# A hybrid SSD / RWKV-7 encoder layer on one core: the state space norm's weight factors folded into the output weight's rows, its token factors multiplied in on GpSimd, four empty turns behind the first load, and the group norm's second product tied behind the chain's

## The chip, the cores and the metric

The kernel runs on one core of a Trainium2 chip. That core has a matrix engine (TensorE, PE in the profile), a vector engine (VectorE, DVE), a scalar engine (ScalarE, ACT), a general engine (GpSimd, POOL), a queue engine that issues nearly all transfers here (SyncE, SP; its instruction stream is "SPq" in the trace) and 16 DMA engines. Each engine executes its own instructions strictly in the order in which they were written into its stream; an instruction that waits holds up everything behind it. The metric is the device time of one execution in microseconds (us); the median of three runs counts.

## What is computed

One layer over 2,048 tokens of width 1,024. One projection feeds two groups of heads: a bidirectional Mamba-2 state space model (SSD, 512 channels) and a bidirectional RWKV-7 recurrence (512 channels). Their outputs side by side go through one 1024x1024 output projection, and an MLP follows. The parts that matter here:

```python
# end of ssd_bidir: RMS norm over each half (256 channels), times a weight per channel
y = (y * silu(z)).reshape(b, T, G, SSD_WIDTH // G)
y = y * rsqrt(mean(y * y, -1, keepdims=True) + RMS_EPS)
y_ssd = y.reshape(b, T, SSD_WIDTH) * norm_g
# end of rwkv7_bidir: group norm over each head of 64 channels
mu_y = mean(y, -1, keepdims=True);  var_y = mean(square(y - mu_y), -1, keepdims=True)
y = ((y - mu_y) * rsqrt(var_y + GN_EPS)).reshape(b, T, W) * lnx_g + lnx_b
y_rwkv = (y + bonus) * g
# hybrid_mixer
mix = concatenate([y_ssd, y_rwkv], -1) @ w_out
h = layer_norm(ALPHA * h + mix, ln1_g, ln1_b)
h = layer_norm(ALPHA * h + square(relu(h @ w_fc)) @ w_proj, ln2_g, ln2_b)
```

Products are made in fp32 precision from halves: an operand x is split into xh (rounded by ScalarE) and xl = x - xh, and three products (xh·wh, xh·wl, xl·wh) are summed in PSUM.

## The kernel before

Three stretches follow one another: projections and state space scan (to about 1,050 us), the RWKV stretch (about 1,060 to 1,970 us), and the MLP (to the end). The change touches the second alone.

The RWKV stretch runs through 32 *units* u (16 chunk pairs for two groups of heads). `weave(chain(u), jobs)` writes the instructions: after each step of `chain(u)`, the serial recurrence, it draws steps from the jobs beside it: `finish(u - 1)` (group norm of finished chunks), `merge(u + 1)`, `inverse(u + 2)` (a triangular inverse, row by row, all on GpSimd: lines 1059 to 1066) and `prep(u + 3)`. Such a job is an entry with a number of steps to be drawn per unit (12 for `finish`).

The chain of one unit makes, twice (c = 0, 1), three small products on PE (all on line 1150, told apart by their operands): `ch<-zv,kr`, then `ch<-rs,nm` (rs is ScalarE's negated copy, line 1166), then `ch<-zv,bkt`; the last one's result is added on VectorE to the state: `zt` (line 1189) at c = 1. The next unit of the same group starts from zv, made from zt.

Between those products, `dense(ins, n)` fills PE with large ones: it adds n to a credit and, while the credit is 1 or more, draws a *piece* of three 128x512 matmuls from `out_pieces`, and ties it behind the given instruction with `tc.issue_after`. A piece generator that yields `HELD` ends that turn and caps the credit at 1. `out_pieces` makes, in this order: gates for blocks 1 and 2; `weights(0)`, which loads the first 512 rows of w_out and splits them (woh, wol; lines 807 and 808); the state space norm's token factors (rt, written to DRAM as rsD, line 891); then the *first pass* of the output projection over 16 token tiles, 8 pieces each, in `products` (line 838); then `weights(4)`, gates for blocks 0 and 3, and the *second pass* for the RWKV half.

`load(t, k.yS, True)` fetches a token tile of the unnormed state space output for the first pass (yr from yS, line 818), fetches the factors of its 128 tokens broadcast over partitions (rsb from rsD, line 821), and scales yr by the weight's factor per channel and the token's factor with four VectorE instructions (line 823). ScalarE then rounds it to yh (line 825) and GpSimd makes yl (line 827). The load for tile j+1 is written when tile j's products begin. In `weights`, ppc(k, "ng", i // 2) would be the column of `norm_g` that belongs to the row block i // 2: partitions there are channels, as they are in yr.

In `finish`, each of two chunks per unit takes a centring product (line 1223), a copy ye (1224) and a square sq on ScalarE (1226), a second product over sq for the variance (line 1230, vp), and then sd (1233), reciprocal and the rest.

What order these streams end up in is decided by a scheduler that goes by an estimated timeline and takes every instruction as soon as its inputs and the ties allow; a small edit can so move rows of all engines.

Of the kernel before, what the change touches and what calls it, by code (L numbers as in the profile page):

```python
# [11 lines left out]
AF = mybir.ActivationFunctionType  # L12
ALU = mybir.AluOpType
# [3 lines left out]
P = 128  # L17
# [23 lines left out]
C_ID, C_MU, C_ML, C_MLX, C_ONE, C_BLK, C_HSEL, C_N = 0, 128, 256, 384, 512, 640, 768, 770  # L41
# [75 lines left out]
FL = 0.4  # L117
FH = 1.0
# [84 lines left out]
def ppc(k, name, j):  # L203
    c = _PP[name] + j
    return k.pp[:, c:c + 1]
# [576 lines left out]
DENSE, HELD, LAST, END = "dense", "held", "last", object()  # L782


def out_pieces(k):


    nc, tc, I = k.nc, k.tc, k.I
    with ExitStack() as ctx:
# [3 lines left out]
        def weights(c0):  # L793
            wh, wl = [cp.tile([P, 4, D], F32R, name=n) for n in ("woh", "wol")]

            def raw(i):
                w = wk.tile([P, 4, P], F32, name="yr").rearrange("p a t -> p (a t)")
                r = (c0 + i // 2) * P
                nc.sync.dma_start(w, I["w_out"][r:r + P, 512 * (i % 2):512 * (i % 2) + 512])
                return w  # L800

            w = raw(0)
            yield
            for i in range(8):
                nxt = raw(i + 1) if i < 7 else None
                cs = wh[:, i // 2, 512 * (i % 2):512 * (i % 2) + 512], wl[:, i // 2, 512 * (i % 2):512 * (i % 2) + 512]
                nc.scalar.copy(cs[0], w)
                nc.gpsimd.tensor_tensor(cs[1], w, cs[0], ALU.subtract)
                w = nxt
                yield  # L810
            k.wo = wh, wl

        def load(t, ys, first):
            h = wk.tile([P, D], F32, name="h")
            nc.sync.dma_start(h, k.hD[t])
            yr = wk.tile([P, 4, P], F32, name="yr")
            for g in range(2):
                nc.sync.dma_start(yr[:, 2 * g:2 * g + 2], ys[g][:, :, P * t:P * t + P].rearrange("a p t -> p a t"))
            if first:
                rsb = wk.tile([P, 2, P], F32, name="rsb")  # L820
                nc.sync.dma_start(rsb, rsD[:, t].unsqueeze(0).broadcast_to([P, 2, P]))
                for c in range(4):
                    nc.vector.scalar_tensor_tensor(yr[:, c], yr[:, c], ppc(k, "ng", c), rsb[:, c // 2], ALU.mult, ALU.mult)
            yh = wk.tile([P, 4, P], F32R, name="yh")
            nc.scalar.copy(yh, yr)
            yl = wk.tile([P, 4, P], F32R, name="yl")
            nc.gpsimd.tensor_tensor(yl, yr, yh, ALU.subtract)
            return t, h, yh, yl
# [63 lines left out]
        yield  # L892
        order = [t for s in range(NT // 2, NT) for t in (NT - 1 - s, s)]
        ops = load(order[0], k.yS, True)
        for j in range(NT):
            nxt = load(order[j + 1], k.yS, True) if j + 1 < NT else None
            yield
            yield from products(ops, True)
            ops = nxt
# [8 lines left out]
        for n, parts in (("ln1_g", (("gh", 512), ("gl", 512))), ("ln1_b", (("b1", 512), ("rsb", 256), ("rsb", 256)))):  # L908
            row, c = [], 0
# [26 lines left out]
def phase_rwkv(k):  # L936
    nc, tc, I = k.nc, k.tc, k.I
    with ExitStack() as ctx:
# [23 lines left out]
        hsl = lambda h: slice(64 * h, 64 * h + 64)  # L962
# [173 lines left out]
        def chain(u):  # L1136
# [8 lines left out]
            def product(lhs, rhs):  # L1145

                k.ch ^= 1
                out = CH[:, k.ch]
                for pr, d, h in pairs_of:
                    mm = nc.tensor.matmul(out[hsl(h), d, pr], lhs(d, pr, h), rhs(d, pr, h), start=True, stop=True)  # L1150
                return out, mm


# [62 lines left out]
        def finish(u):  # L1216

            pg, fin = u % 2, FIN.pop(u)
            yield
            sds = []  # L1220
            for nat, ya in fin:
                cp_ = k.ps.tile([P, 2, P], F32, name="ps")
                nc.tensor.matmul(cp_, rc[:, R_CEN:R_CEN + P], ya, start=True, stop=True)
                (nc.scalar.copy if CA else nc.vector.tensor_copy)(ya, cp_)
                sq = wk.tile([P, 2, P], F32, name="sq")
                nc.scalar.activation(sq, cp_, AF.Square)
                yield
                yield
                vp = k.ps.tile([P, 2, P], F32, name="ps")
                nc.tensor.matmul(vp, k.cst[:, C_BLK:C_BLK + P], sq, start=True, stop=True)  # L1230
                yield
                sd = sm.tile([P, 2, P], F32, name="sd")
                nc.scalar.activation(sd, vp, AF.Sqrt, bias=k.eps[:, 2:3], scale=1.0 / 64)
                for pr in range(2):
                    nc.vector.reciprocal(sd[:, pr], sd[:, pr])
                sds.append(sd)
            for (nat, ya), sd in zip(fin, sds):
                tok = slice(P * nat, P * nat + P)
                bon = wk.tile([P, 2, P], F32, name="bon2")
                nc.sync.dma_start(bon, pairs(k.bD[pg][:, :, tok]))  # L1240
                gate = wk.tile([P, 2, P], F32, name="gate")
                nc.sync.dma_start(gate, pairs(k.gD[pg][:, :, tok]))
                yield
                nc.vector.tensor_tensor(ya, ya, sd, ALU.mult)
                for pr in range(2):
                    p = 2 * pg + pr
                    if TA:
                        nc.scalar.activation(ya[:, pr], ya[:, pr], AF.Identity, scale=ppc(k, "lnx_g", p), bias=ppc(k, "lnx_b", p))
                    else:
                        nc.vector.tensor_scalar(ya[:, pr], ya[:, pr], ppc(k, "lnx_g", p), ppc(k, "lnx_b", p), ALU.mult, ALU.add)  # L1250
                yield
                nc.gpsimd.tensor_tensor(bon, ya, bon, ALU.add)
                o = wk.tile([P, 2, P], F32, name="o")
                (nc.gpsimd if OG else nc.vector).tensor_tensor(o, bon, gate, ALU.mult)
                nc.sync.dma_start(pairs(k.yR[pg][:, :, tok]), o)
                k.final[nat] += 1
# [29 lines left out]
        for u in range(-AH, U):  # L1286
            jobs = []
            if 0 <= u - 1 and FIN[u - 1]:
                fin = finish(u - 1)
                if FE:  # L1290
                    next(fin)
                jobs.append((fin, 12, FL, FH, 0))
            if 0 <= u + MG < U:
                jobs.append((merge(u + MG), 5, ML, 0.9, PM))
            if 0 <= u + AH - 1 < U:
                jobs.append((inverse(u + AH - 1), 16, IL, IH, PI))
            if u + AH < U:
                jobs.append((prep(u + AH), 18, 0.0, PH, PP_))
            k.u = u
            jobs.append((k.ssd, SR, 0.0, 1.0, PS))  # L1300
            weave(chain(u) if u >= 0 else iter([None] * 12), jobs)
# [388 lines left out]
```

## Time and profile before

| | us |
|---|---|
| three runs | 3348.42, 3336.12, 3338.42 |
| median | 3338.42 |
| profiled execution: time | 3344.93 |
| profiled execution: span of the trace | 3343.1 |
| PE busy in the span | 2994.1 (90%) |
| VectorE busy | 2183.9 (65%) |
| GpSimd busy | 1563.2 (47%) |
| ScalarE busy | 1526.6 (46%) |
| mean granted TensorE clock | 0.921 of full speed |

The trace has rows of several kinds. A row of the timeline starts with the time in us from the span's start and the duration, then engine, line, operation, "output<-inputs", partitions x elements and how many alike were put together; in brackets stands how long the engine was idle before it and what ended that wait. A row of the waits has: who waited, for what; us in total, how often, the longest. A row of a window has its bounds, its length, PE's busy time with the number of matmuls, the granted clock (1.00 is full speed), the DMA engines' busy share and GB/s. A row of the groups has busy time, mean ns of one, and the idle time before it with what ended it.

### The profile page before, as it was taken

To read this page: it belongs to the slowest core of one execution; us is meant where nothing else is said; L and a number is where in the kernel's file an instruction comes from. 1 tells how busy PE (TensorE), PEld (TensorE's weight loads), DVE (VectorE), ACT (ScalarE), POOL (GpSimd) and SP (SyncE) were. 2 spreads that over 40 slices of the span, in tenths; PEclk is the share of its full clock that TensorE was granted. 3 is DMA by queue.
4 is the path that set the end of the run, shared out by engine and by line. 5 is a ranking of instruction groups with operands and counts; after the bars stand their busy time and mean duration, and the time that the engine had idled before them with its cause. 6 is when DMAs were issued, how large, how long until landed. Compare 5 with 4: busy or idle time off the path is not lost. (4 is left out here: it accounts for less than half of the span.)

```text
span 3343.1 us, 63829 instructions
## 1 busy us (share of the span) xinstructions
PE 2994.1 (90%) x23783; PEld 2396.2 (72%) x23783; DVE 2183.9 (65%) x3703; ACT 1526.6 (46%) x2961; POOL 1563.2 (47%) x1940
## 2 busy tenths in 40 slices
PE   5879999988887799998889885999899989999997
PEld 3767877776675577776677664888787868887885
DVE  7798556676666455565567768767887744466455
ACT  3556323333334444455556545544544553444332
POOL 0352124444445333334466655554576335556645
PEclk9989999889996688888789987999999999999998
DMA  6445355786778566666565444777799475566554
GB/s 208 134 157 184 123 152 175 195 223 188 211 209 256 143 162 160 161 159 175 147 168 152 126 156 143 245 242 233 260 327 310 139 301 198 190 215 213 193 198 151
DMA packets 711287, 641.84 MB, mean 192 GB/s; under 512 B 203552, under 2 KB 561600, under 8 KB 710336
## 3 DMA queue, kind: packets, MB, share of 16 engines
q1 hardware_dynamic: 710976, 637.76, 61.9%
q8 instruction: 187, 3.06, 0.4%
q14 instruction: 124, 1.02, 0.1%
HBM read 399.24 MB, written 238.37 MB: 191 GB/s over the span
## 5 line engine op out<-in xcount | busy, mean ns | idle before, releaser
L1558 DVE TENSOR_TENSOR ul<-ul,uh 128x1024 fp32r<-128x1024 f32 x112 | 247.6, 2213 | 284.6 <-ACT uh L1557 284.4
L1558 POOL TENSOR_TENSOR pl<-pl,ph 128x1024 fp32r<-128x1024 f32 x112 | 291.7, 2608 | 273.6 <-ACT ph L1557 273.4
L1512 PE MATMUL ps<-hh,wh 128*128 128x512 f32 x896 | 352.6, 394 | 21.1 <-ACT wh L1375 7.7
L266 PE MATMUL psg<-hh,wh 128*128 128x512 f32 x864 | 357.1, 414 | 9.0 <-ACT u L285 8.1
L1616 PE MATMUL ps<-ph,uh 128*128 128x512 f32 x896 | 348.5, 392 | 10.5 <-ACT ph L1557 6.3
L268 PE MATMUL psg<-hl,wh 128*128 128x512 f32 x864 | 353.8, 410 | 1.4 <-DVE hl L236 1.4
L267 PE MATMUL psg<-hh,wl 128*128 128x512 f32 x864 | 354.8, 411 | 0.0
L1616 PE MATMUL ps<-pl,uh 128*128 128x512 f32 x896 | 349.7, 391 | 5.3 <-POOL pl L1558 5.3
L1512 PE MATMUL ps<-hh,wl 128*128 128x512 f32 x896 | 351.2, 392 | 2.5 <-DVE wl L1376 2.5
L1512 PE MATMUL ps<-hl,wh 128*128 128x512 f32 x896 | 350.9, 392 | 1.4 <-DVE hl L1435 1.4
L1616 PE MATMUL ps<-ph,ul 128*128 128x512 f32 x896 | 348.1, 389 | 0.0
L1376 DVE TENSOR_TENSOR wl<-wa,wh 128x512 fp32r<-128x512 f32 x217 | 211.5, 979 | 85.4 <-ACT wh L1375 84.5
L1557 ACT CAST ph<-pl 128x1024 fp32r<-128x1024 f32 x112 | 117.7, 1051 | 288.3 <-DMA pl<-pD 282.4
L1065 POOL TENSOR_TENSOR ltmp<-ln,la 128x30 f32<-128x30 f32 (+10 forms) x480 | 123.1, 257 | 263.6 <-DMA la<-ad 232.5
L1375 ACT CAST wh<-wa 128x512 fp32r<-128x512 f32 x217 | 132.8, 618 | 209.3 <-POOL wa L1348 100.1
L1512 PEld LDWEIGHTS ps<-hh,wh 128*128 128x128 f32 x896 | 169.8, 189 | 60.5 <-ACT wh L1375 9.0
L266 PEld LDWEIGHTS psg<-hh,wh 128*128 128x128 f32 x864 | 169.8, 197 | 49.4 <-ACT u L285 9.5
L1616 PEld LDWEIGHTS ps<-ph,uh 128*128 128x128 f32 x896 | 169.1, 189 | 47.0 <-ACT ph L1557 7.2
L1616 PEld LDWEIGHTS ps<-pl,uh 128*128 128x128 f32 x896 | 169.0, 189 | 43.3 <-POOL pl L1558 8.5
L1512 PEld LDWEIGHTS ps<-hh,wl 128*128 128x128 f32 x896 | 169.6, 189 | 38.0 <-DVE wl L1376 3.0
L268 PEld LDWEIGHTS psg<-hl,wh 128*128 128x128 f32 x864 | 168.5, 195 | 39.4 <-issue 3.1
L1512 PEld LDWEIGHTS ps<-hl,wh 128*128 128x128 f32 x896 | 169.6, 189 | 37.8 <-DVE hl L1435 1.8
(322 smaller groups left out, 7059.4 us busy)
## 6 DMA issues: line engine op xcount, KB each, us to landing
uD<-ua SPq DMA_DIRECT2D x224, 256.0 KB, 2.8
ul<-uD SPq DMA_DIRECT2D x112, 512.0 KB, 4.6
pl<-pD SPq DMA_DIRECT2D x112, 512.0 KB, 3.8
wa<-in_w_fc_dram SPq DMA_DIRECT2D x124, 256.0 KB, 3.3
pD<-sc SPq DMA_DIRECT2D x112, 256.0 KB, 4.1
rk<-rk SPq DMA_DIRECT2D x64, 384.0 KB, 4.7
h<-hD SPq DMA_DIRECT2D x48, 512.0 KB, 3.5
eD<-et SPq DMA_DIRECT2D x32, 514.0 KB, 2.7
```

The costliest lines, as they stand in the source:

```text
L266: nc.tensor.matmul(pt, wh[:, c], hh[:, c], start=(c == 0), stop=False)
L267: nc.tensor.matmul(pt, wl[:, c], hh[:, c], start=False, stop=False)
L268: k.lag = nc.tensor.matmul(pt, wh[:, c], hl[:, c], start=False, stop=(c == KC - 1))
L1065: eng.tensor_tensor(tv, ln[:, 0:m, r:r + 1].broadcast_to([P, m, w]), la[:, r:r + 1, r + 1:16].broadcast_to([P, m, w]), ALU.mult)
L1375: nc.scalar.copy(hi, x)
L1376: nc.vector.tensor_tensor(lo, x, hi, ALU.subtract)
L1512: nc.tensor.matmul(pt, x, y, start=(n == 0 and i not in (2, 3)), stop=(n == 11 and i not in (1, 5)), skip_group_check=True)
L1557: nc.scalar.copy(hi, x)
L1558: eng.tensor_tensor(lo, x, hi, ALU.subtract)
L1616: nc.tensor.matmul(banks[j], x, z, start=(g == 0 and s == 0), stop=(g == NG - 1 and s == 5))
```

## The change

Four edits, all in the RWKV stretch:

1. In `weights(0)`, for the first 512 rows of w_out, ScalarE multiplies each loaded 128x512 block by norm_g of its rows before the split: 8 instructions more.
2. In `load(..., first=True)` the four VectorE instructions per tile become one GpSimd multiplication of the whole 128x512 tile by rsb: 64 VectorE instructions less, 16 GpSimd instructions more.
3. After the first load of the first pass, `out_pieces` yields `HELD` four times.
4. In `finish` one more step is yielded between the square and the second product, that product is tied behind the last matmul that the chain had written by then (`k.tie`), and the job's steps per unit go from 12 to 14.

```diff
@@ weights
+                if c0 == 0:
+                    nc.scalar.activation(w, w, AF.Identity, scale=ppc(k, "ng", i // 2), bias=0.0)
                 nc.scalar.copy(cs[0], w)
                 nc.gpsimd.tensor_tensor(cs[1], w, cs[0], ALU.subtract)
@@ load
                 nc.sync.dma_start(rsb, rsD[:, t].unsqueeze(0).broadcast_to([P, 2, P]))
-                for c in range(4):
-                    nc.vector.scalar_tensor_tensor(yr[:, c], yr[:, c], ppc(k, "ng", c), rsb[:, c // 2], ALU.mult, ALU.mult)
+                ys = yr.rearrange("p (g c) t -> p g c t", g=2)
+                nc.gpsimd.tensor_tensor(ys, ys, rsb.unsqueeze(2).broadcast_to([P, 2, 2, P]), ALU.mult)
@@ out_pieces
         ops = load(order[0], k.yS, True)
+        for _ in range(4):
+            yield HELD
@@ chain, product
-                    mm = nc.tensor.matmul(out[hsl(h), d, pr], lhs(d, pr, h), rhs(d, pr, h), start=True, stop=True)
+                    mm = k.tie = nc.tensor.matmul(out[hsl(h), d, pr], lhs(d, pr, h), rhs(d, pr, h), start=True, stop=True)
@@ finish
                 yield
                 yield
+                yield
                 vp = k.ps.tile([P, 2, P], F32, name="ps")
-                nc.tensor.matmul(vp, k.cst[:, C_BLK:C_BLK + P], sq, start=True, stop=True)
+                with tc.issue_after(k.tie.ins):
+                    nc.tensor.matmul(vp, k.cst[:, C_BLK:C_BLK + P], sq, start=True, stop=True)
@@ phase_rwkv
-                jobs.append((fin, 12, FL, FH, 0))
+                jobs.append((fin, 14, FL, FH, 0))
```

New lines shift the numbers: 815 to 827 of before are 818 to 830 of after (the scaling, 823, is 826 and on GpSimd), 838 is 841, 1059/1065/1066 are 1064/1070/1071, 1150 is 1155, 1189 is 1194, 1223 and 1230 are 1228 and 1237.

**VectorE in the steady first pass.** The first pass spends one token tile per unit; in each of these units VectorE's stream has the scaling of the next tile between a transposition for the merge and the chain's zt. Before:

```order
L1097 STREAM_TRANSPOSE n_15405<-dd 128x256
L823 SCALAR_TENSOR_TENSOR yr<-yr,pp,rsb 128x128 x4
L1189 TENSOR_TENSOR zt<-zz_14952,ch 128x256
L1192 TENSOR_TENSOR zv<-zt,dtab 64x4x64 x2
L1193 TENSOR_TENSOR zz_15162<-zt,dtab 128x256
```

The same unit's place after:

```order
L1102 STREAM_TRANSPOSE n_15364<-dd 128x256
L844 SCALAR_TENSOR_TENSOR h<-h,psg 128x512
L1194 TENSOR_TENSOR zt<-zz_14913,ch 128x256
L1197 TENSOR_TENSOR zv<-zt,dtab 64x4x64 x2
L1198 TENSOR_TENSOR zz_15121<-zt,dtab 128x256
```

The four scalings are gone; the addition of half a tile's products to h (line 841 before, 844 now), which stood behind zz, now stands ahead of zt.

**GpSimd in the same units.** Before, between one inverse and the next and early in the next:

```order
L1066 TENSOR_TENSOR ln<-ln,ltmp 128x8
L1059 COPY ln<-rc 128x128
L1065 TENSOR_TENSOR ltmp<-ln,la 128x15
L1066 TENSOR_TENSOR ln<-ln,ltmp 128x15
L1065 TENSOR_TENSOR ltmp<-ln,la 128x14
L1066 TENSOR_TENSOR ln<-ln,ltmp 128x14
L1065 TENSOR_TENSOR ltmp<-ln,la 128x26
L1066 TENSOR_TENSOR ln<-ln,ltmp 128x2x13
L827 TENSOR_TENSOR yl<-yr,yh 128x512
```

After (yl then stands some twenty rows later, near the inverse's end):

```order
L1071 TENSOR_TENSOR ln<-ln,ltmp 128x8
L826 TENSOR_TENSOR yr<-yr,rsb 128x512
L1064 COPY ln<-rc 128x128
L1070 TENSOR_TENSOR ltmp<-ln,la 128x15
L1071 TENSOR_TENSOR ln<-ln,ltmp 128x15
```

The scaling stands at the seam between two inverses, ahead of the row step that needs la; in some units it stands behind the copy of line 1064 instead of ahead of it.

**PE where the first pass begins** (ip is a step of the merge, nm its operand). Before:

```order
L1130 MATMUL ip<-nm_9564,t_10575 32x32 x7
L838 MATMUL psg<-woh,yh 128x512
L838 MATMUL psg<-wol,yh 128x512
L1130 MATMUL ip<-nm_9564,t_10575 32x32 x9
L1033 MATMUL ps<-cst,bk 128x64 x3
L838 MATMUL psg<-woh,yl 128x512
```

Nine more of line 838 and one of line 1033 follow, and then `ch<-zv,kr`. After:

```order
L1135 MATMUL ip<-nm_9564,t_10555 32x32 x16
L841 MATMUL psg<-woh,yh 128x512
L841 MATMUL psg<-wol,yh 128x512
L1038 MATMUL ps<-cst,bk 128x64 x4
L1155 MATMUL ch<-zv,kr 64x64
L841 MATMUL psg<-woh,yl 128x512
L1155 MATMUL ch<-zv,kr 64x64 x7
```

The first dense products stand at nearly the same place; between them and the chain's next product stand three instead of twelve.

**PE around one second product of the group norm** (the 17th of 32). Before, and then after:

```order
L1150 MATMUL ch<-zv,bkt 64x64 x8
L1199 MATMUL yp<-ra,zv 64x64 x7
L1109 MATMUL ip<-dd,t_21223 32x32 x21
L1230 MATMUL ps<-sq,cst 128x256
L1223 MATMUL ps<-ye,rc 128x256
L1109 MATMUL ip<-dd,t_21223 32x32 x11
L838 MATMUL psg<-woh,yh 128x512
L1150 MATMUL ch<-zv,kr 64x64 x8
```

```order
L1155 MATMUL ch<-zv,kr 64x64 x8
L1228 MATMUL ps<-ye,rc 128x256
L841 MATMUL psg<-woh,yh 128x512
L841 MATMUL psg<-wol,yh 128x512
L841 MATMUL psg<-woh,yl 128x512
L841 MATMUL psg<-woh,yh 128x512
L841 MATMUL psg<-wol,yh 128x512
L841 MATMUL psg<-woh,yl 128x512
L1177 MATMUL yp<-kr,zv 64x64 x8
L1127 MATMUL ip<-n_21229,at 32x32 x6
L1237 MATMUL ps<-sq,cst 128x256
```

It stood ahead of the chain's `ch<-zv,kr`; now that product and two pieces stand ahead of it. The 21st stood after five of the eight matmuls of `ch<-rs,nm` and now stands after seven of them:

```order
L1155 MATMUL ch<-rs,nm_9566 64x64 x7
L1237 MATMUL ps<-sq,cst 128x256
L1228 MATMUL ps<-ye,rc 128x256
L1155 MATMUL ch<-rs,nm_9566 64x64
L841 MATMUL psg<-woh,yh 128x512
```

## The prediction

> **What bounds the kernel now.** I read the page's first two parts, then PE's waits and clock stretch by stretch.
>
> ```profile
> PE 2994.1 (90%) x23783; PEld 2396.2 (72%) x23783; DVE 2183.9 (65%) x3703; ACT 1526.6 (46%) x2961; POOL 1563.2 (47%) x1940
> PE   5879999988887799998889885999899989999997
> PEclk9989999889996688888789987999999999999998
> ```
>
> PE is busy 90% of the span, and both PE and its clock are worst in slices 13 to 25, the RWKV stretch (a slice is 83.6 us). There, windows over PE (length, busy, clock): the first twelve units that spend a token tile of the first pass, the two that follow, and two single units of the twelve, the first and the third.
>
> ```profile
> 1149.40:1464.40 315.00, 293.43 (x5137) 0.84 0.61 157
> 1464.40:1507.30 42.90, 42.15 (x857) 1.00 0.70 174
> 1149.40:1176.90 27.50, 25.45 (x429) 0.81 0.56 150
> 1200.90:1228.70 27.80, 26.37 (x429) 0.75 0.58 148
> ```
>
> Twelve units take 26.25 us each, the next two 21.45 with the same 429 matmuls per unit. What differs is that in those two no tile is scaled any more (the sixteen tiles are loaded ahead). If twelve units went at 21.45, they would take 257.4: 57.6 less. That excess splits by the busy column: 293.43 - 12 x 21.08 = 40.5 us are slower matmuls (clock), the other 17 are idle. What ends the idle time, by the waits from 1142 to 1540:
>
> ```profile
> PE ch L1150 <- DVE zt L1189: 18.3, 11, 3.4
> PE psg L838 <- ACT yh L825: 17.1, 1, 17.1
> PE ch L1150 <- ACT rs L1166: 5.0, 1, 5.0
> DVE yr L823 <- DMA yr<-yS: 38.7, 14, 5.9
> ```
>
> PE's chain waits for zt, and VectorE stands at the scaling until its transfer lands. One unit in the timelines of VectorE and PE:
>
> ```profile
> 1380.75 0.69 PE L1150 MATMUL ch<-zv,bkt 128*64 128x64 f32 x16
> 1383.06 1.27 DVE L823 SCALAR_TENSOR_TENSOR yr<-yr,pp,rsb 128x128 f32<-128x128 f32 x4 [3.14 <-DMA yr<-yS]
> 1384.25 0.41 DVE L1189 TENSOR_TENSOR zt<-zz,ch 128x256 f32<-128x256 f32 x1
> ...
> 1384.72 0.69 PE L1150 MATMUL ch<-zv,kr 128*64 128x64 f32 x16 [0.66 <-DVE zt L1189]
> 1387.35 1.16 PE L1019 MATMUL ps<-kr,bk 64*128 64x128 f32 x16
> ```
>
> zt adds the product that PE ended at 1381.4; VectorE was idle then, but held by the scaling, so zt ran at 1384.25 and PE stood 0.66 us. That small gap left the clock alone: 16 matmuls of line 1019 took 1.16 us after it. A longer one did not:
>
> ```profile
> 1191.04 1.16 PE L1019 MATMUL ps<-kr,bk 64*128 64x128 f32 x16
> 1200.12 0.69 PE L1150 MATMUL ch<-zv,kr 128*64 128x64 f32 x16 [2.22 <-DVE zt L1189]
> 1203.00 2.08 PE L1019 MATMUL ps<-kr,bk 64*128 64x128 f32 x16
> ```
>
> After 2.22 us of idle the same 16 took 2.08 us, and the unit from 1200.9 has a clock of 0.75. So a late zt is paid twice, and the clock is the larger part.
>
> **The change, term by term.** Prices are from the profiled execution of 3344.93 us, which lies 6.5 us over the median of 3338.42.
>
> *Scaling off VectorE.* 64 instructions leave, one longer one per tile arrives on GpSimd; the nearest row for it is yl, the same 128x512 with two inputs.
>
> ```profile
> L823 DVE SCALAR_TENSOR_TENSOR yr<-yr,pp,rsb 128x128 f32<-128x128 f32 x64 | 20.5, 374 | 66.4 <-DMA yr<-yS 38.7 <-DMA rsb<-rsD 15.9 <-POOL ln L1066 8.1
> L827 POOL TENSOR_TENSOR yl<-yr,yh 128x512 fp32r<-128x512 f32 x32 | 41.6, 1303 | 27.9 <-ACT yh L825 24.2 <-DMA yo<-yaD 3.7
> ```
>
> Ahead of zt VectorE then has a half tile's addition to h; in the changed order its last matmul stands on PE directly ahead of the product that zt adds, so it can run beside that product. The idle 18.3 us and the clock that follows it come back: 40.5 less the 4.4 us of the first unit (its busy time, 25.45, follows another wait), so 36. Together 54; some gaps remain (PE also waits for rs, 5.0), and I take -50. Bounds: -18 if only the idle comes back, -58 if all twelve units go at 21.45.
>
> On GpSimd the instruction stands at the seam of two inverses, ahead of the row step that waits for la.
>
> ```profile
> 1390.52 0.29 POOL L1059 COPY ln<-rc 128x128 f32<-128x128 f32 x1 [5.77 <-DMA nd<-ln]
> 1399.47 0.21 POOL L1065 TENSOR_TENSOR ltmp<-ln,la 128x15 f32<-128x15 f32 x1 [8.66 <-DMA la<-ad]
> ...
> POOL ltmp L1065 <- DMA la<-ad: 18.6, 2, 9.8
> POOL ln L1059 <- DMA nd<-ln: 8.9, 2, 5.0
> ```
>
> The last two rows are the waits of 1464 to 1507, the two units at 21.45: even there GpSimd is idle 9.3 us per unit for la and 4.5 for nd. 1.3 us, and a wait for yr, disappear in these 13.8; the scaling costs nothing there. Without the cover it is 16 x 1.3 = 21 us. Queued behind it are the copy of ln, the inverse's rows and through them nd, ni and the merge; and yl now stands near the inverse's end, so the yr buffer comes free later and the next load is issued later. A tile is scaled a unit or more ahead of its products, which leaves room. If a stall comes next, it is the one for rs.
>
> *Two inputs on VectorE beside GpSimd.* Two rows of the same pair of multiplications, the first beside a 128x512 GpSimd operation, the second without:
>
> ```profile
> 1805.51 2.65 DVE L1007 TENSOR_TENSOR bk<-bk,E 128x256 f32<-128x256 f32 x2 [0.57 <-PE ps L1033]
> 1387.17 0.75 DVE L1007 TENSOR_TENSOR bk<-bk,E 128x256 f32<-128x256 f32 x2
> ```
>
> 1.9 us longer. Sixteen such meetings at no more than 1.3 us of GpSimd work each bound it at 0 and +21; VectorE has lost 20.5 us itself and most meetings fall outside the short path to zt: +3. The Trainium skill ("SBUF — State Buffer", "Who interferes with whom") says that a VectorE instruction with two SBUF inputs and a GpSimd instruction that reads SBUF exclude each other for their whole length; by that rule alone each scaling could hold VectorE for its full time, and the sum would be 18 us worse than by mine. This case's row agrees with the direction of it (2.65 beside 0.75).
>
> *Factors in the weight.* Eight 128x512 activations on ScalarE; the nearest row is another in-place scaling of that shape.
>
> ```profile
> L1498 ACT ACTIVATE ua<-ua 128x512 f32<-128x512 f32 x96 | 60.6, 632 | 79.3 <-DVE ua L1497 77.2
> PE ps L1033 <- ACT bkt L1035: 8.6, 4, 4.0
> ACT woh L807 <- DMA yr<-in_w_out_dram: 3.7, 3, 2.9
> ```
>
> 8 x 0.63 = 5.1 us of work between 1040 and 1110, where PE already waits 8.6 us for a ScalarE copy (second row, PE's waits there), but ScalarE also stands 3.7 us for the weight's transfer (third row), which the new work can run behind. +2, between 0 and +5.1.
>
> *Four turns.* The wait that opens the first pass:
>
> ```profile
> 1121.15 0.25 ACT L889 COPY rt<-ps 32x128 f32<-32x128 f32 x1
> ...
> 1133.12 0.55 SPq L1069 DMA_DIRECT2D nd<-ln  x1
> 1133.76 0.57 SPq L891 DMA_DIRECT2D rsD<-rt  x1
> ...
> 1142.30 0.80 PE L838 MATMUL psg<-woh,yh 128*128 128x512 f32 x1 [17.09 <-ACT yh L825]
> ...
> 1148.63 0.68 PE L1150 MATMUL ch<-zv,kr 128*64 128x64 f32 x16
> ```
>
> The factors were ready at 1121.4, but their store is queued on SP behind an inverse's nd, and went out at 1133.76; then come the broadcast, the scaling, yh, and PE. In the changed order SP's stream reads the same there, and PE's first dense product stands at nearly the same place. So I leave the 17 us where they are (bounds -17 and 0). Behind it three dense matmuls precede the chain instead of twelve: of the 6.3 us to 1148.63 some 4.7 go, and nine matmuls come later, where they cost nearly the same unless they fill idle time: -2, between -4.7 and 0.
>
> *The second product.* From 1540 to 1972 PE waits for sq, and so does whatever stands behind:
>
> ```profile
> PE ps L1230 <- ACT sq L1226: 14.4, 6, 6.2
> ...
> 1812.11 0.70 PE L1230 MATMUL ps<-sq,cst 128*128 128x256 f32 x2 [2.87 <-ACT sq L1226]
> ...
> 1812.10:1818.90 6.80, 6.79 (x51) 0.57 0.60 172
> ...
> 1874.09 1.22 PE L1230 MATMUL ps<-sq,cst 128*128 128x256 f32 x2 [6.22 <-ACT sq L1226]
> 1876.10 0.69 PE L1150 MATMUL ch<-rs,nm 64*64 64x64 f32 x6
> ```
>
> In the new order the one at 1812 (the 17th) has the chain's next product and two pieces ahead of it: its 2.87 us and about 3 us of clock (6.8 us at 0.57) should go. The one at 1874 (the 21st) still has the last matmul of the chain's product behind it, because the tie names the product that the chain had written when the job's step was drawn, an earlier one; its 6.22 us stay. Two at the very end have no chain behind them. -6; bounds 0 and -21 (14.4 and two clock losses of 3.4). sd and its reciprocal come later, which only yR reads.
>
> Sum: -50 + 3 + 2 - 2 - 6 = -53. 3344.93 - 53 = 3291.9; at the median's level, 6.5 lower, 3285.
>
> **Rivals.**
>
> 1. *The idle time goes, the slow clock stays*, since it falls for other reasons or at gaps of other origin. Then the first term is -18: -21 in all, 3317. Against it: the clock fell right behind gaps of this wait, and stayed at 1.00 through the two units without scaling. By the rule in the Trainium skill ("TensorE: Matmul & The Clock Gate", "What's actually happening") the clock drops after an idle window of about 3.4 us; only the longest of the eleven waits comes near that, and this rival would be the outcome. The trace disagrees: 2.22 us of idle stand ahead of a unit at 0.75.
> 2. *GpSimd becomes the late one* (the other side). Place: the scaling's wait for yr at the seam; the later yl delays the buffer, the load, and the next scaling in a circle. Nothing happens up to 13.8 us of blocking per unit; 4 us beyond that, over fifteen units, is +60 and holds the chain as zt did, with the same clock: 3345 to 3365. It decides from about 3.5 us beyond the cover. For it: the transfer's wait was up to 5.9 us on VectorE; against: that is less than half of the cover.
> 3. *VectorE and GpSimd collide in full*: +21 instead of +3, 3303.
> 4. *The turns do remove the opening wait* (the store of rsD gets ahead): 17 us more, 3268. Against: SP's order.
> 5. *The second half is reshuffled into new stalls*: each like the one at 1874 costs 6.2 and 3.4 of clock; four new ones are +38, 3323. The edits move rows on every engine there; nothing in the profile says which way.
> 6. *The tie does nothing*: -47 instead of -53, 3291, inside the likeliest case's range.
>
> **How the numbers follow.** Chances: my forecast (with 6) 0.58, its own range 3268 to 3305; rival 1 0.12, rival 2 0.06, rival 3 0.08, rival 4 0.06, rival 5 0.10. The lower end: rival 4 with some of the sq bound, 3260. The upper end takes in rivals 1 and 3 and half of 5: 3321. Left out are rival 2, half of 5 and the tails. 0.5% (16.7 us) is about what a measurement of this kernel tells from no change. Faster, below 3321.7: 0.58 + 0.08 + 0.06, 0.09 of rival 1, 0.04 of rival 5, rounded to 0.84; slower: 0.04 of rival 2, 0.02 of rival 5; the rest is the same.
>
> **What the changed profile would show.** Right: units of about 21.5 to 22 us between 1150 and 1490 at a clock near 1.00; no wait of PE for zt longer than 1 us; GpSimd's wait for la shorter by about the scaling's time; the 17 us in front of the first dense product still there; a wait for sq of about 6 us in the second half, but fewer of them. Wrong: clock stretches without gaps of PE (rival 1); a wait of GpSimd for yr with la's gone, or of VectorE for ni (rival 2); VectorE multiplications of over 1 us beside each scaling (rival 3).

## The result: 3380.28 us, 1.15% slower

| | before | changed |
|---|---|---|
| median of 4 runs | 3337.73 us | 3380.28 us |
| range | 3336.12 to 3348.42 | 3379.51 to 3382.05 |
| span of the profiled execution | 3343.1 | 3377.7 |

The ratio is 1.0115, with a 95% interval of 1.0097 to 1.0134. A loss of about 43 us stands where a gain of 53 was forecast.

The page of the changed kernel, first two parts:

```profile
PE 2981.8 (88%) x23783; PEld 2380.6 (70%) x23783; DVE 2158.2 (64%) x3639; ACT 1529.8 (45%) x2969; POOL 1577.8 (47%) x1956
PE   5879999988886788887888886999899989999997
PEclk9989999999986888888898987999999999999998
```

PE is busy 12 us less than before in a span that is 35 us longer. In slices 13 to 19 the clock is a little better (one slice has 8 where it had 6, the others are alike), and PE's busy share is worse (8 in slices 15 to 18, where it was 9): idle time took the place of slow matmuls. By a window over the first pass, from the end of one product of the chain to the end of the same product sixteen units later, before and then changed:

```profile
1149.40:1569.00 419.60, 387.12 (x6849) 0.85 0.61 158
```

```profile
1150.30:1593.20 442.90, 376.84 (x6852) 0.87 0.59 148
```

23 of the 35 us arise here. The second half of the RWKV stretch, to the same product of the last unit, takes 388.2 us instead of 383.8, and what follows, mostly the MLP, 6 us more (over all kernels below it varies between 1388 and 1399 with no edit in it). PE's waits from 1142 to 1540 in the changed kernel:

```profile
PE ch L1155 <- ACT rs L1171: 50.4, 13, 7.2
PE psg L841 <- ACT yh L828: 17.1, 1, 17.1
```

The wait for zt is gone, as forecast, and a longer one for rs has its place. The waits of ScalarE and of SP in the same window, before and then changed, lead on from there:

```profile
ACT vrev L1040 <- DMA rk<-rk: 13.1, 3, 9.1
ACT vrev L1045 <- DMA rk<-rk: 106.7, 14, 11.2
```

```profile
SPq L818 <- POOL ltmp L1065: 20.8, 11, 4.0
SPq L821 <- POOL ln L1071: 69.9, 8, 9.6
SPq L821 <- POOL ltmp L1070: 37.1, 4, 10.8
```

ScalarE stands 107 us at vrev, a copy of the loaded tile rk, and rs is behind it in its stream; before, that was 13.1 us. SP stands 107 us at the yr load. One unit, on SP, GpSimd, ScalarE and PE of the changed kernel (nd is the inverse's result on its way to DRAM and ni its reload; ad and la are the store and the reload of what the next inverse needs):

```profile
1396.02 0.33 SPq L851 DMA_DIRECT2D hD<-h  x1
1404.58 0.87 SPq L821 DMA_DIRECT2D yr<-yS  x2
1405.61 0.55 SPq L1074 DMA_DIRECT2D nd<-ln  x1
1406.26 0.57 SPq L818 DMA_DIRECT2D h<-hD  x1
1406.91 0.91 SPq L1219 DMA_DIRECT2D yaD<-ye  x2
1407.88 0.56 SPq L1074 DMA_DIRECT2D nd<-ln  x1
1408.49 0.70 SPq L1002 DMA_DIRECT2D rk<-rk  x1
...
1417.88 2.02 SPq L1061 DMA_DIRECT2D la<-ad  x2
```

```profile
1403.28 1.27 POOL L830 TENSOR_TENSOR yl<-yr,yh 128x512 fp32r<-128x512 f32 x1
...
1405.38 0.21 POOL L1071 TENSOR_TENSOR ln<-ln,ltmp 128x8 f32<-128x8 f32 x1
```

```profile
1413.88 0.40 ACT L1045 COPY vrev<-rk 128x256 f32<-128x256 f32 x1 [6.49 <-DMA rk<-rk]
1414.73 0.38 ACT L1171 ACTIVATE rs<-ch 128x256 f32<-128x256 f32 x1
```

```profile
1415.17 0.68 PE L1155 MATMUL ch<-rs,nm 64*64 64x64 f32 x16 [2.53 <-ACT rs L1171]
```

yl, which now stands near the inverse's end, ends at 1404.55; only then is its yr buffer free, and the yr load, at which SP has stood for 8 us, goes out at 1404.58. Behind it in SP's stream stand nd, h, the stores of ye, rk and the rest. rk goes out at 1408.49, ScalarE gets it at 1413.88, and PE has waited. In this unit the yr load can have held rk for about 1 us only: nd, ahead of rk, stores the inverse's result, which was ready at 1405.59. What the hold did to the rest of SP's stream is taken up at the run with the yr loads on GpSimd's queue.

### The profile page after: what moved, and what is told of

It reads as the page before. It is cut to its first block, busy times and chain, and to the rows that moved or that the text cites. A ratio compares the mean times of both kernels' runs of the same rounds, so it can differ in the third digit from the quotient of the medians.

```text
span 3377.7 us, 63746 instructions
## 1 busy us (share of the span) xinstructions
PE 2981.8 (88%) x23783; PEld 2380.6 (70%) x23783; DVE 2158.2 (64%) x3639; ACT 1529.8 (45%) x2969; POOL 1577.8 (47%) x1956
## 5 line engine op out<-in xcount | busy, mean ns | idle before, releaser
L1519 PEld LDWEIGHTS ps<-hh,wl 128*128 128x128 f32 x896 | 169.9, 190 | 36.4 <-DVE wl L1383 1.4
```

Source lines behind the costliest of these rows:

```text
L1519: nc.tensor.matmul(pt, x, y, start=(n == 0 and i not in (2, 3)), stop=(n == 11 and i not in (1, 5)), skip_group_check=True)
```

## The experiments

Two theories to begin with. Theory 1: the four turns shift the load against the inverse, so that yl stands late on GpSimd, and SP is blocked at the yr load. Theory 2: the scaling on GpSimd makes the load and the chain late by itself. The order bears on it: with the turns yl stands after 25 or 26 of the inverse's 30 row operations, without them after 6, whoever scales.

Stretches of single profiles differ by themselves. In the first pass the kernel before, the tie alone and the additional step alone have their rows in the same order on every engine to about 1,500 us, and take 419.6, 415.7 and 412.9 us; a difference of 7 us there tells nothing. In the second half the order changes with every edit, wherever the edit is, and it takes 371 to 402 us over the kernels below. The ratios are from several executions each and are given with their intervals.

**Factors and scaling alone.** The change without the turns and the tie (shortened; the additional step and the 14 go as well):

```diff
-        for _ in range(4):
-            yield HELD
-                with tc.issue_after(k.tie.ins):
```

> Norm factors in the weight's rows and token scaling on GpSimd, without the four turns and without the tied second product; yl stands early in the inverse again (after 6 of its 30 row steps, as before; 25 or 26 in the changed kernel). Theory 1 (the four turns put yl late on GpSimd, the next yr load then waits for its buffer on SP, and rk is queued behind it): SP's wait for GpSimd at the yr load stays near 20 us in the first pass, ScalarE's wait for rk under 20 us, PE's wait for zt goes from 18 to under 5 us; 3280 to 3310 us. Theory 2 (the scaling on GpSimd itself makes the load and the chain late): PE's waits for rs of 40 us or more as in the changed kernel, 3365 to 3385 us.

3348.11 us, ratio 1.002 (1.0003 to 1.0037). Neither theory: it isn't as slow as the change, and it isn't fast. The wait for zt is gone and rs is waited for 31 us, again behind rk:

```profile
PE ch L1153 <- ACT rs L1169: 31.2, 13, 4.3
```

```profile
ACT vrev L1043 <- DMA rk<-rk: 90.6, 15, 8.4
```

**The turns alone.**

```diff
+        for _ in range(4):
+            yield HELD
```

> Only the four empty turns behind the first load; scaling stays on VectorE in four instructions. yl stands late in the inverse (25 or 26 of 30 row steps). Theory 1: SP waits 80 us or more for GpSimd at the yr load in the first pass, ScalarE 80 us or more for rk, PE 40 us or more for rs; 3365 to 3395 us. Theory 2: no such waits, within 10 us of before (3328 to 3348).

3385.16 us, 1.0128 (1.0106 to 1.015): as much as the change loses, from one edit that adds no instruction. In its profile 21 of 39 us arise in the first pass (441.0 us), and 18 in the second half (401.7), where the edit can act only by a new order of the rows. SP waits 98 us for GpSimd at the yr load. The consumer that shows it is another than I expected: scaling is still on VectorE here, and the late yr holds VectorE (91.3 us), then ScalarE and PE (50.9 us for bkt).

```profile
DVE yr L823 <- DMA yr<-yS: 91.3, 15, 8.2
```

```profile
PE ps L1035 <- ACT bkt L1037: 50.9, 12, 5.7
```

**The tie alone** (shortened; `k.tie` is set in the chain as in the change).

```diff
+                yield
+                with tc.issue_after(k.tie.ins):
-                jobs.append((fin, 12, FL, FH, 0))
+                jobs.append((fin, 14, FL, FH, 0))
```

> Only the tied second product with its additional step and 14 steps per unit; the first pass reads as before on GpSimd and SP. Both theories: the first pass is as before (315 us for its twelve units within 5); the wait for sq falls from 14.4 to about 10 us; 3325 to 3342 us.

3364.5 us, 1.0051 (1.0026 to 1.0076). Slower, not faster: the second half takes 395.8 us, 12 more than before.

**A third yr buffer in the changed kernel** (the same at the two other places that make this tile).

```diff
-            yr = wk.tile([P, 4, P], F32, name="yr")
+            yr = wk.tile([P, 4, P], F32, name="yr", bufs=3)
```

> The changed kernel with three buffers for yr instead of two: yl still stands late in the inverse, but the yr load no longer needs the buffer that this yl reads. Theory 1: SP's wait at the yr load falls from 107 us to under 30, ScalarE's wait for rk from 107 to under 30, PE's wait for rs from 60 to under 15; 3290 to 3320 us. Theory 2: the waits for rs stay at 40 us or more and the time at 3365 to 3385.

3357.29 us, 1.0029 (1.0009 to 1.0048), between the two ranges. It tells the theories apart less than I meant: SP still waits 90 us for GpSimd at the yr load (the order moved the load a tile ahead, to where it again needs a buffer whose yl is late), and rs is still waited for 54 us. From the second of the sixteen units on, the first pass takes 418.8 us, as in the change (419.0). What it won against the change lies at the start of the first pass, where the wait for yh fell from 17.1 to 8.1, and in the second half.

**No turns in the changed kernel.**

```diff
-        for _ in range(4):
-            yield HELD
```

> The whole change without the four turns: yl early in the inverse as before. Theory 1: the first pass as in ab_only, the second half as in tie_only; 3350 to 3368 us, some 20 us faster than the whole change. Rival (the turns cost only by themselves and gain beside the scaling): 3375 us or more.

3365.9 us, 1.0059 (1.0037 to 1.008): by the two ratios 0.56% faster than the change, some 19 us; the first pass takes 420.7 us (413.1 in the version with factors and scaling alone), the second half as much as with the tie alone (395.7). The costs don't add up: the turns alone, the tie alone, and factors and scaling alone lose 1.28, 0.51 and 0.20%, together 1.99, and the change loses 1.15.

**The yr loads from GpSimd's own queue.** There the load stands right behind the yl that frees its buffer, and holds up nobody else.

```diff
-                nc.sync.dma_start(yr[:, 2 * g:2 * g + 2], ys[g][...])
+                (nc.gpsimd if first else nc.sync).dma_start(yr[:, 2 * g:2 * g + 2], ys[g][...])
```

> The whole change, with the yr loads of the first pass issued from GpSimd's queue, behind the yl that frees their buffer, so that they no longer hold up SP. Theory 1 (SP blocked at the yr load makes rk late): SP's wait of 107 us at that load is gone, ScalarE's wait for rk falls from 107 to under 60 us (the loop through nd stays), 3345 to 3365 us. Rival P: waits for rk and rs as in the changed kernel, 3375 to 3390 us.

3362.31 us, 1.0052 (1.0036 to 1.0068). The first pass goes from 442.9 to 407.2 us, while yl stays as late as it was, and PE, VectorE and ScalarE have their rows of the steady pass in the order of the change:

```profile
1145.80:1553.00 407.20, 362.81 (x6851) 0.90 0.64 161
```

So the turns cost the first pass through SP's stream, not through the shift of the products. But rk is still waited for 87 us (I expected under 60), and the second half took 402.4. And half of SP's wait only moved, since nd has to wait for the inverse in any case:

```profile
SPq L1074 <- POOL ln L1071: 56.2, 14, 9.0
```

Theory 1 is right in the place and not in the way. rk goes out 3.6 us after the inverse's end in the kernel before and in the change alike (means of twelve and eleven steady units). What the held yr load moves is the group around it: in the unit shown, the load itself, h and rsb crowd in about the inverse's end, ahead of la; before, yr and h were out by then. From the yr load to la 17 issues stand there; before, in the like place, 14, of which these are the first and the last:

```profile
1384.36 0.36 SPq L821 DMA_DIRECT2D rsb<-rsD  x1
...
1395.19 2.23 SPq L1056 DMA_DIRECT2D la<-ad  x2
```

la goes out 10.9 us after the inverse's end before, 12.4 in the change and 6.7 here; from one inverse to the next it is 26.0, 28.0 and 24.6 us. This is read from the traces; no run moves those transfers alone.

What theory 1 leaves open is why factors and scaling alone gain nothing. In that version one round trip can be read off SP and GpSimd:

```profile
1263.97 1.22 SPq L1072 DMA_DIRECT2D nd<-ln  x2
1265.29 0.57 SPq L1000 DMA_DIRECT2D rk<-rk  x1
1266.81 1.56 SPq L1075 DMA_DIRECT2D ni<-nd  x2
1268.48 1.40 SPq L1053 DMA_DIRECT2D ad<-at  x2
1271.99 2.00 SPq L1059 DMA_DIRECT2D la<-ad  x2
...
1288.31 1.22 SPq L1072 DMA_DIRECT2D nd<-ln  x2
```

```profile
1276.16 0.21 POOL L1068 TENSOR_TENSOR ltmp<-ln,la 128x15 f32<-128x15 f32 x1 [9.00 <-DMA la<-ad]
...
1288.07 0.21 POOL L1069 TENSOR_TENSOR ln<-ln,ltmp 128x8 f32<-128x8 f32 x1
```

SP waits for the inverse to end before it can store nd; ni waits for nd to land; ad, needed for the inverse of a later unit, is queued behind both; la waits for ad; the next inverse waits 9 us for la, runs 12 us, and nd goes out 24.3 us after the last one. Theory L: this loop through SP's in-order queue sets the pace of the first pass, and rk, in the same queue, is late with it. The units of 21.45 us, on which the prediction rests, would then be two units that lived on tiles loaded ahead.

**nd and ni from GpSimd's queue,** with factors and scaling, and in the kernel before:

```diff
-                nc.sync.dma_start(nd[:, :, q], ln[64 * q:64 * q + 64])
+                nc.gpsimd.dma_start(nd[:, :, q], ln[64 * q:64 * q + 64])
-                nc.sync.dma_start(ni[hsl(h)], ...)
+                nc.gpsimd.dma_start(ni[hsl(h)], ...)
```

> As ab_only (factors in the weight, scaling on GpSimd, no turns, no tie), and the inverse's store nd and its reload ni are issued from GpSimd's own queue instead of SP's; the order of all other rows is unchanged. Theory L (the first pass is bound by a loop of about 25 us through SP's in-order queue: nd waits for the inverse, ad and rk are queued behind nd and ni, la waits for ad, the next inverse for la): ScalarE's wait for rk falls from 91 to under 20 us, PE's for rs from 31 to under 8, the units of the first pass to 21.5 to 23 us; 3285 to 3315 us. Rival P (the rk transfers themselves, or the DMA engines, are late, or transfers issued by GpSimd cost its rows as much): waits for rs stay above 25 us, 3335 us or more.

> The kernel before with nd and ni issued from GpSimd's queue; scaling on VectorE. Theory L: VectorE's wait for yr shrinks in part, as SP reaches the yr load and the rest earlier; units of 23 to 26 us, 3300 to 3335 us. Rival P: no change or slower, 3335 to 3360 us.

3323.97 us, 0.9932 (0.991 to 0.9954), and 3322.52 us, 0.9929 (0.9906 to 0.9953). Through the steady first pass, from about 1190 to 1470 us, the other rows stand in the order of the kernels that these two come from, but for loads of bk on SP in the first. Sixteen units take 389.9 and 386.4 us instead of 413.1 and 419.6:

```profile
1151.20:1541.10 389.90, 356.95 (x6849) 0.94 0.65 169
```

```profile
1149.10:1535.50 386.40, 363.62 (x6849) 0.92 0.64 171
```

With the queue free, it makes no difference which engine scales. The first missed its range (3285 to 3315): rk is still waited for 51 us.

**One more GpSimd operation inside the inverse,** in the kernel before and with nd and ni from GpSimd's queue (shortened):

```diff
+                if r == 5 and 3 <= u <= 16:
+                    eng.tensor_tensor(scr, scr, ln (broadcast), ALU.mult)   # 128x512
```

> The kernel before with one 128x512 GpSimd multiplication more (on a scratch tile of zeros, about 1.3 us) in the middle of the inverse of 14 units; nothing waits for its result. GpSimd is idle 10 us and more per unit there. Theory L (the inverse lies on the loop nd, ad, la, inverse): each unit is about 1.3 us longer, 14 x 1.3 = 18 us and a loss of clock, 3352 to 3380 us. Rival (idle time on GpSimd is cover): within 8 us of before.

> The same additional GpSimd multiplication in the kernel that issues nd and ni from GpSimd's queue. Theory L: the loop through SP is open, so the 1.3 us cost little: within 8 us of that kernel without it (3322), 3316 to 3332 us. Rival (the additional work costs by itself, by port or clock): as much more as in the kernel before, 3338 us or more.

3346.17 us, 1.0 (0.9983 to 1.0017), and 3323.94 us, 0.9925 (0.9898 to 0.9952): nothing in either, where theory L had +18 us or more for the first. The first doesn't decide, since SP's order also changed there (nd in one piece, rk ahead of bk): la goes out 9.0 us after the inverse's end instead of 10.9, and from one inverse to the next it is 26.0 us as before, the inverse 1.3 longer and the rest 1.3 shorter. In the second the other engines' rows of the steady pass stand in the order of the kernel without the operation, whose ratio is 0.9929: with nd and ni off SP, GpSimd's idle time covers it.

**The whole change with all three off SP** (nd, ni and the yr loads from GpSimd's queue).

> The whole change with nd, ni and the first pass's yr loads all issued from GpSimd's queue: neither the inverse nor the late yl holds up SP. Theory 1 with theory L: the late yl costs nothing any more, ScalarE's wait for rk under 50 us, units of the first pass at 22 to 24 us; what is left is the tied product's cost in the second half: 3325 to 3350 us. Rival (the four turns cost by the shift of the dense products, not through SP): 3355 us or more.

3340.24 us, 0.998 (0.9962 to 0.9999): the loss of the change is gone. PE waits 21.5 us for a ScalarE-fed copy of zv on VectorE in the first pass instead of 50.4 for rs.

**Factors and scaling with the same three off SP.**

> Factors in the weight and scaling on GpSimd, without turns and tie; nd, ni and the yr loads from GpSimd's queue. A version that could beat both: SP's remaining wait of 45 us for GpSimd at the yr load goes. Theory L: 3305 to 3325 us, at or below the 3324 of the version with nd and ni alone. Rival (GpSimd's queue becomes the bound, since it waits for nd to land before each ni): 3325 us or more.

3320.3 us, 0.9912 (0.9879 to 0.9945).

**No scaling at all,** in the kernel before and with nd and ni from GpSimd's queue. These two leave the norm's factors out, and with them the transfers of rsb:

```diff
-            if first:
-                rsb = wk.tile([P, 2, P], F32, name="rsb")
-                ...
-                    nc.vector.scalar_tensor_tensor(yr[:, c], yr[:, c], ppc(k, "ng", c), rsb[:, c // 2], ALU.mult, ALU.mult)
```

> The kernel before with the first pass's scaling left out altogether (no factors, no rsb transfer; the first pass multiplies unnormed data). Theory Q (SP's in-order stream, in which the loads stand behind nd, sets the pace, whichever engine scales): the 16 units of the first pass take 405 to 420 us (419.6 before), 3325 to 3348 us. The prediction's own step (a unit takes 21.5 us once nothing is scaled on VectorE): 16 units near 360 us, 3275 to 3295 us.

> No scaling, and nd and ni issued from GpSimd's queue. Theory Q: as the same with scaling (386 us for the 16 units, 3322 us) within 12 us: 3308 to 3326 us. Rival (with SP free, the scaling is the next bound): 16 units under 365 us, below 3300 us.

3342.3 us, 0.9974 (0.9953 to 0.9995), and 3278.25 us, 0.9797 (0.976 to 0.9833). This pair answers the main question. Take the scaling away altogether, and the kernel before gains 0.3%; its sixteen units take 423.7 us, no fewer than with scaling, and ScalarE now waits for rk as it did in the version that scales on GpSimd:

```profile
ACT vrev L1035 <- DMA rk<-rk: 91.6, 14, 11.7
```

Free SP as well, and six units in a row take 21.1 us each at full clock:

```profile
1228.30:1354.90 126.60, 126.23 (x2569) 1.00 0.72 188
```

There are two limits side by side: the late yr that holds VectorE, and the inverse's transfers that hold SP. Taking one away shows the other; taking both away gives the pace that the prediction assumed. (The time of the second run fell on the rival's side of what I expected: with SP free, the scaling is the next limit. Its sixteen units, 371.6 us, lie between the two forecasts.) This holds for leaving the scaling out, not for moving it to GpSimd: with SP free that gave 0.9932, as on VectorE, and 0.9912 with the yr loads off SP too. What holds these two back is not isolated.

**rk from ScalarE's queue,** with factors and scaling on GpSimd:

```diff
-                nc.sync.dma_start(rk, pairs(k.rk[pg][:, :, tok]))
+                nc.scalar.dma_start(rk, pairs(k.rk[pg][:, :, tok]))
```

> As ab_only, with the rk loads issued from ScalarE's queue instead of SP's; nd, ni, ad and la stay on SP, all other rows as in ab_only. Theory Q (rk is late because it is queued behind nd): ScalarE's wait for rk falls from 91 to under 40 us, PE's for rs from 31 to under 12, 16 units 385 to 400 us, 3318 to 3335 us. Theory L (the loop nd, ad, la, inverse): PE waits elsewhere instead, 16 units 408 to 418 us, 3338 to 3355 us.

3348.71 us, 0.9996 (0.9977 to 1.0015). ScalarE's wait for rk is down to 3.8 us, and the merge's nm waits for ni instead; PE, which had waited 31.2 us for rs, now waits 36.4 for nm:

```profile
ACT nm L1119 <- DMA ni<-nd: 38.5, 10, 6.9
PE ip L1125 <- ACT nm L1119: 36.4, 12, 5.8
```

So rk was a symptom; what is late is the whole group of transfers that stand behind the inverse on SP. Here theory L is right in kind; its sixteen units took 423.0 us, a little over its range.

**The additional step without the tie.**

```diff
+                yield
-                jobs.append((fin, 12, FL, FH, 0))
+                jobs.append((fin, 14, FL, FH, 0))
```

> The additional step in the group norm's job and 14 steps per unit, without the tie. If the later place in the job's sequence makes the cost of tie_only: 3355 to 3370 us. If the tie itself does: 3335 to 3350 us, as before.

3359.25 us, 1.004 (1.0017 to 1.0063); the second half takes 399.5 us. The step and the job's new pace cost by themselves about what the tie alone cost (1.0051, 1.0026 to 1.0076); a cost of the tie beside them isn't shown. Which of the moved rows costs it stays open. The turns alone, which leave this job as it was, have 401.7 us in the second half, so a new order there is enough; the whole change shows 388.2.

**Two versions on the way to the free pace.** The kernel before with nd and ni from GpSimd's queue, and the yr loads either there too or with a third buffer:

> The kernel before, scaling on VectorE, with nd, ni and the first pass's yr loads issued from GpSimd's queue (the yr load stands right behind the yl that frees its buffer). If the late load is what is left: VectorE's wait for yr falls to under 15 us, 16 units 372 to 382 us, 3290 to 3312 us. If it is GpSimd's blocked queue or the scaling's transfers themselves: 3315 to 3330 us, as with nd and ni alone.

> The kernel before with nd and ni issued from GpSimd's queue and three buffers for yr, so that the load need not wait for the last tile's yl. If the late load is what is left: 16 units 372 to 382 us, 3290 to 3312 us; otherwise 3315 to 3330 us.

3341.67 us, 0.9971 (0.9951 to 0.9992), missed: VectorE is still held at the scaling, for 39 us by what the profile puts down to GpSimd (28.4 and 11.0) and for 9 by yr's transfer, and SP now waits 73 us at the load of the residual rows h for an earlier store of them to land. The faster of the two has 33 us of the first and 31 of the last, so the wait at h is the likelier cause; no run isolates it. And 3309.53 us, 0.9897 (0.9843 to 0.995), with VectorE's wait for the transfer of yr down to 4.2 us and, in its profile, sixteen units at the pace of no scaling:

```profile
1147.90:1520.10 372.20, 349.55 (x6845) 0.96 0.67 178
```

That profile is the fastest of four executions (3294 to 3329), and the one without scaling the slowest of its four (3275 to 3297); by the medians there is still 1% between the two. This version has the lowest ratio of those that leave nothing out, 1.0% faster than the kernel before, though its interval overlaps those of the versions at 0.991 to 0.993; and none of the four edits of the change is in it.

## Why the prediction was wrong

- *What bounds the kernel.* That VectorE's scaling holds zt was read rightly, and zt's wait went from 18.3 us to nothing in the first pass. The step that failed is the next: "If twelve units went at 21.45". That pace was taken from two units and used as the pace of all; it made the term of -50, nearly the whole of the -53. The trace of before had the sign against it, on ScalarE in the second of those two units:

```profile
1496.82 0.41 ACT L1040 COPY vrev<-rk 128x256 f32<-128x256 f32 x1 [3.24 <-DMA rk<-rk]
```

  rk was already late there, and the wait for rs of 5.0 us, of which I wrote "If a stall comes next, it is the one for rs", was the same thing one unit on. In those two units no tile is scaled, as I said; SP also has no load of yr and rsb in them. And the loop that makes the inverses did not speed up with PE: while PE's two units took 21.45 us each, nd went out on SP 24.8 and 25.1 us apart.

```profile
1463.66 0.54 SPq L1069 DMA_DIRECT2D nd<-ln  x1
...
1488.41 0.54 SPq L1069 DMA_DIRECT2D nd<-ln  x1
...
1513.53 0.55 SPq L1069 DMA_DIRECT2D nd<-ln  x1
```

  So PE used up a lead there, and the pace could not last. Leaving the scaling out altogether is worth nothing in the kernel as it stands (419.6 and 423.7 us), where I had -50; with nd and ni off SP as well, the two together are worth 48 us (371.6). Moving it to GpSimd was worth nothing either way (413.1 beside 419.6, which is within what like profiles differ by, and 389.9 beside 386.4).
- *GpSimd's cover.* "1.3 us, and a wait for yr, disappear in these 13.8; the scaling costs nothing there." No run shows a cost of the 1.3 us. But the idle time that I counted as cover is the latency of the round trip nd, ad, la, in which SP waits. I asked what was queued behind the scaling on GpSimd, and not what was queued behind the yr load on SP.
- *The late yl.* I wrote that "the next load is issued later" and "a tile is scaled a unit or more ahead of its products, which leaves room". The tile had room; what had none was SP, where the held load pushes other transfers into the round trip from nd to la. In the profile 23 of the 35 us are lost in this pass, and they belong to the turns: 442.9 us with them, 420.7 without.
- *Four turns.* Priced at -2, with bounds of -4.7 and 0 beside the opening wait; measured alone: +1.28%, some 43 us, of which its profile has about half in the first pass. The opening wait of 17.1 us stayed, as forecast. What I priced was the burst of products; what counts is that the turns moved the load by a third of a unit against the inverse, for the whole pass.
- *Rival 2* had the sign (the later yl, the buffer, the load), and a chance of 0.06. Its place was wrong: it looked for the stall on GpSimd, where the cover is, and not on SP.
- *Rival 1, the clock.* It didn't decide: the idle time did not go. The clock of the pass stayed low with the new gaps (0.87, before 0.85), and was 1.00 where there were none (the six units above).
- *Two inputs on VectorE.* +3. The scaling on GpSimd took 1.30 us each, and beside the sixteen of them six VectorE rows were longer than their like: kr 0.90 and 0.98 us instead of 0.42, ao 0.91 to 1.42 instead of 0.69.

```profile
1351.36 1.42 DVE L1096 TENSOR_TENSOR ao<-at,rc 128x512 f32<-128x512 f32 x1
```

  That is some 3 us in all, the size that I gave it; whether it reached the end time isn't shown.
- *Factors in the weight.* +2, between 0 and +5.1. ScalarE took 0.72 us for each instead of 0.63, 5.8 us in all, and PE's wait for bkt from 1040 to 1110 went from 8.6 to 13.9 us: just over the upper end.
- *The second product.* -6 with 0 as the worse bound; alone it cost 0.5%. As forecast, the waits for sq fell (from 14.4 to 6.9 us), and the one of 6 us behind the chain's product stayed (6.1). But other waits came in the second half: for zt 8.3 us where it was 1.6, for the merge's t 6.7 where it was 0.7. That the reordering could cost was in rival 5, not in the term's bounds.

## What to carry to other kernels

Before the pace of a few undisturbed iterations is taken as what a loop can do, look whether they live on work done ahead: the first late transfer in or right after them tells. When an instruction moves, list for each queue what stands behind the transfer that waits for it, above all on the engine that issues transfers; a wait there is charged to whatever is next, and removing its consumer only changes the name in the list of waits. Two limits of nearly the same length are found by removing both, not by removing each. And when two profiles are compared by a stretch, first look how much the stretch differs between profiles whose rows there are alike.

## What the runs showed of the hardware

Moving four small transfers per unit (nd and ni, two of 32 KB each) from one issuing engine to another was worth 0.7%, though their issue takes GpSimd 1.4 us for a pair, and though GpSimd then stands some 5 us before it can issue ni: it had the time, and SP had not. And with those transfers on GpSimd, a 128x512 operation more per unit there cost nothing measurable (0.9925, 0.9898 to 0.9952, beside 0.9929, 0.9906 to 0.9953).
